# Scaling the first pooled weights by sums of all squares instead of column norms in a hybrid attention and pooling layer

## The chip, the cores and the metric

The kernel runs on one core of one Trainium2 chip. The metric is the device time of one execution in microseconds. Before the change it is 1169.89 us, the median of three runs that lie between 1169.45 and 1170.81.

## The reference

One encoder layer on 4096 tokens of 1024 channels, all in float32:

```
h = rmsnorm(x, pre_norm_g)
[q | k | v | g_a | u_p | g_p] = h @ w_in          # 2304 columns
a = banded_attention(q, k, v, rel_bias, sink) * silu(g_a)   # |i-j| <= 128, 8 heads
p = multiscale_pool(u_p, pool_w, pool_scale) * silu(g_p)    # windows 2, 4, 8, 16
x = x + rmsnorm(concat(a, p) @ w_out, post_norm_g)
```

The change touches how the kernel prepares the weights of `g_p`, the gates of the pooling half (512 columns of `w_in`), and of the normalization of the first tokens.

## The kernel before, in words

**Numbers.** TensorE multiplies float16. Each float32 operand is split into a high and a low float16 half, and a product takes three matmuls (high by high, low by high, high by low). So that the halves keep their accuracy, every group of weight columns is first multiplied by a power of two, `sw`, which is computed on the chip from the weights: `scale_of` (line 192) turns a bound on the squares into that power in four small instructions. The first gain vector has such a power too, `gs`. The inverse powers come back in the factors that evacuations multiply by (`sc`, `isc`, `cg`, `uf`).

**Stages.** The first stage, to about 470 us, projects the tokens in eight blocks of 512 (m = 0 to 7) on the three groups GP (`g_p`), UU (`u_p` with the pooling map folded in) and GA (`g_a`). Block 0 uses plain products: `plain` (line 743) goes over four quarters of operands, A11, A12, A21 and A22, four steps of six matmuls each for each half of the tokens. Later blocks use seven products of sums of those quarters (`quad`, line 777). The later stages (keys, values, queries, attention, output) have a schedule by hand and aren't touched.

**The planner.** In the first stage every operation is a step, `do(engine, cost, due, function, r=..., w=...)`. `Steps.run` (line 86) takes, for the engine that can begin earliest, the step with the smallest due time among those that are ready, adds its cost and a gap of 0.2 us, and so writes one fixed order for every engine. On the chip the engines run in that order, with semaphores between them. Costs and due times are thus only what makes the order. A square of a tile costs `act(D)`, 1.10; a low half `dve(D)`, 1.33.

**The opening.** ScalarE squares the first 256 tokens, transposed, in four chunks (`first_square`, line 416); VectorE adds the chunks in three additions and a fold (`first_add`, `first_fold`, lines 419 to 423); two matmuls with a column of ones sum over the channels (`first_sum`, 425), VectorE adds the epsilon (`first_eps`, 433), GpSimd takes the power -1/2 (`first_root`, 436), TensorE spreads the result over all partitions (`spread`, 442). Then, for each chunk c, VectorE normalizes (`norm_half`, 478: two instructions of 128x256), ScalarE makes the high half (`b_high`, 494) and VectorE the low half (`b_low`, 497).

Ahead of that stands the gain: its largest square is found (`gain_most`, `gain_spread`), and `gain_scale` (394) reduces it, makes `gs`, and scales the gain (`gsc`) and a factor (`gh`).

The weights of GP come in four tiles; tiles 0 and 1 are group "ga" (operands A11 and A12), tiles 2 and 3 group "gb" (A21 and A22). In `norms` (590) ScalarE squares a tile (`w_square`, 567), eight matmuls with ones sum the squares of each of its 128 columns over the 1024 rows (`w_norm`, 573), and `w_scale` (582) takes the largest of the 256 column sums of the group with a reduction of 128x256 (`scale_pow`, 186), makes `sw`, and then `sc` and `isc`. With `sw`, ScalarE writes the high half of each operand (`w_high`, 605) and VectorE the low half (`w_low`, 608). Until weights and tokens are there, TensorE runs idle matmuls (`turn_over`, 402: 52, then 40, then 24 of them).

`gp_flags` (662) later brings both groups of GP to their smaller power, `com`, for the sums of later blocks, and makes the factor `uf` from it. At the end of the first stage `out_scales` (1121) puts `isc` into the rows of the output weights.

The steps of the prediction name these: the "second scale" is that of group "gb"; the "fourth low half of x" is `b_low` of chunk 3.

Of the kernel before, what the change touches and what calls it, by code (L numbers as in the profile page):

```python
# [8 lines left out]
F32 = mybir.dt.float32  # L9
# [8 lines left out]
P = 128  # L18
# [116 lines left out]
def hybrid_layer(ctx: ExitStack, tc, io, out):  # L135
# [75 lines left out]
    with ExitStack() as actx:  # L211
# [55 lines left out]
        def tile_keys(q, si):  # L267
            a = si // 2
            return [f"tile{q}.{si}"] + raw_keys(q, 2 * a) + raw_keys(q, 2 * a + 1)
# [14 lines left out]
        def dve(n):  # L284
            return 0.1 + n * 0.0012
# [11 lines left out]
        def t_scalar(eng, out, in0, s1, op0, s2=None, op1=None):  # L297
            if op1 is None:
                eng.tensor_scalar(out=out, in0=in0, scalar1=s1, scalar2=None, op0=op0)
            else:  # L300
                eng.tensor_scalar(out=out, in0=in0, scalar1=s1, scalar2=s2, op0=op0, op1=op1)
# [89 lines left out]
            bc["g"] = spread_tile(P, 0)  # L391
            nc.tensor.matmul(bc["g"], bc["m"].to_broadcast([P, P]), ident, start=True, stop=True)

        def gain_scale():
            m2 = comm.tile([P, 1], F32, name="m2", tag="m2")
            V.tensor_reduce(out=m2, in_=bc.pop("g"), axis=mybir.AxisListType.X, op=ALU.max)
            scale_of(gs, m2, 1e-30, H_SCALE)
            t_scalar(V, gsc, g_pre, gs, ALU.mult)
            t_scalar(V, gh, gs, 1.0 / H_SCALE, ALU.mult)

# [7 lines left out]
        do("PE", 5.5, -9, turn_over, 52, r=["ones"], w=["bankv", "turned"])  # L408
        do("PE", 0.3, -6, gain_spread, r=["ident", "gmost", "turned"], w=["bc", "spread0"])
        do("PE", 2.3, -6, turn_over, 40, r=["ones", "spread0"], w=["bankv"])  # L410
        do("DVE", 1.4, -6, gain_scale, r=["gpre"], w=["gs", "bc"])


        xsq = NT[:, : 2 * D].rearrange("p (k b t) -> p k b t", k=HK, b=2)
# [107 lines left out]
        for c, d in ((0, 1), (2, 3), (1, 3)):  # L522
            do("DVE", dve(512), -4, first_add, c, d, r=[f"xsq{c}"], w=[f"xsq{d}"])
        do("DVE", dve(256), -4, first_fold, w=["xsq3"])
        do("PE", 0.5, -4, first_sum, r=["onesf", "xsq3"], w=["wup1", "summed"])
        do("DVE", 0.2, -4, first_eps, w=["wup1", "ssq0"])
        do("POOL", 0.8, -3, first_root, slice(0, 2), r=["mhalf", "ssq0"], w=["rs0"])
        for i, t, k in ((2, xn1, "xn"), (3, NT[:, 2 * D : 3 * D], "ts")):
            ld(-2.5 + 0.1 * i, t, x_blk[i], 0.5, w=[k])
# [34 lines left out]

        n2_t = {}

        def w_square(raw, z):
            A.activation(
                sqt[z].rearrange("p (g c) -> p g c", g=2) if len(raw.shape) == 3 else sqt[z], raw,
                AF.Square,  # L570
            )

        def w_norm(z, group, i, n, b):
            if i == 0:
                n2_t[group] = psa.tile([P, n, P], F32, name=f"n2{group}", tag=f"n2{b}")
            for k in range(KT):
                nc.tensor.matmul(
                    n2_t[group][:, i], ones16, sqt[z][:, k * P : (k + 1) * P], start=(k == 0),
                    stop=(k == KT - 1), skip_group_check=True,
                )  # L580
# [9 lines left out]
        def norms(keys, last, views, reads, group, cols):  # L590
            n, b = len(views), turn("n2")
            for i, (key, view, r) in enumerate(zip(keys, views, reads)):
                z = turn("sq")
                do("ACT", act(D), key, w_square, view, z, r=r, w=[f"sqt{z}"])
                do("PE", 0.5, key + 0.5, w_norm, z, group, i, n, b,
                   r=["ones", f"sqt{z}"] + ["summed"] * (group == "ga"), w=[f"n2{b}"])
            do("DVE", 1.5, last, w_scale, group, cols, r=["gs"], w=[f"n2{b}", f"sw{group}"])

        def tile_view(q, i):
            return raws[q][:, 2 * (i // 2) : 2 * (i // 2) + 2, i % 2]  # L600
# [25 lines left out]
        def sum_weights(q, scale, group, key, step, eng, again=False):  # L626
# [8 lines left out]
            if again:  # L635
# [10 lines left out]
            pair(q, S2, 0, scale, key + 2.5 * step, group)  # L646
            pair(q, S4, 1, scale, key + 3.5 * step, group)

        norms([5, 5], 5, [tile_view(GP, i) for i in (0, 1)], [tile_keys(GP, i) for i in (0, 1)],
              "ga", slice(0, 2))  # L650
        do("PE", 1.4, 6, turn_over, 24, r=["ones", "swga"], w=["bankv"])
        do("PE", 0.9, 5.6, row_prod, r=["row", "yt0", "summed"], w=["n20"])
        do("ACT", 0.7, 5.6, row_keep, w=["n20", "yt0"])
        for i, op, key in ((0, A11, 9.5), (1, A12, 12.5)):
            pair(GP, op, i, sw[:, 0:1], key, "ga")
        norms([13, 13], 13, [tile_view(GP, i) for i in (2, 3)], [tile_keys(GP, i) + ["w4h"] * (i == 3) for i in (2, 3)],
              "gb", slice(2, 4))

        def gp_gates():
# [2 lines left out]
        def gp_flags():  # L662
            V.reciprocal(rat, sw[:, 0:4:2])
            tt(V, com, sw[:, 0:1], sw[:, 2:3], ALU.min)
            t_scalar(V, rat, rat, com, ALU.mult)
            t_scalar(V, sc[:, 0:4], com.to_broadcast([P, 4]), gh, ALU.mult)
            V.reciprocal(isc[:, 0:4], sc[:, 0:4])
            w_gates(cg[:, 0:4], slice(0, 4))
            t_scalar(V, uf, sc[:, 0:1], U_EVAC * GP_EVAC * H_SCALE, ALU.mult)

        do("DVE", 0.2, 20, gp_gates, r=["swga", "swgb"] + [f"xb0.{c}.1l" for c in range(HK)], w=["gates"])
        do("DVE", 1.2, 40, gp_flags, r=["swga", "swgb", "gates"], w=["flags", "swgc"])
        for i, op, key in ((2, A21, 16.0), (3, A22, 17.0)):
            pair(GP, op, i, sw[:, 2:3], key, "gb")

# [445 lines left out]
        def out_scales():  # L1121


            tt(V, rowsc[:, 0:4], isc[:, A_GA : A_GA + 4],
               isc[:, SB + B_V : SB + B_V + 1].to_broadcast([P, 4]), ALU.mult)
            tt(V, rowsc[:, 4:8], isc[:, A_GP : A_GP + 4], isc[:, A_U : A_U + 4], ALU.mult)
            t_scalar(V, rowsc[:, 0:4], rowsc[:, 0:4], 2.0**25, ALU.mult)
            stt(rowsc[:, 4:8], rowsc[:, 4:8], 2.0**26, psc, ALU.mult, ALU.mult)

# [1014 lines left out]
```

## Time and profile before

| | |
|---|---|
| median of three runs | 1169.89 us (1169.45 to 1170.81) |
| span of the profiled execution, first to last instruction | 1166.3 us |
| median less that span | 3.6 us |
| TensorE busy | 1150.3 us, 99% of the span |
| VectorE busy | 937.0 us, 80% |
| ScalarE busy | 702.3 us, 60% |
| GpSimd busy | 314.2 us, 27% |
| mean granted clock of TensorE | 0.997 |

The page of the profile gives the span of the profiled execution and no time of its own beside it; what lies around the span is therefore taken as the distance to the median. The lines shown below name, for each group or piece, the engine, the line of the kernel, the operation, what it writes and reads, the shape, and how many there were. In the order of time the first two numbers are the start and the duration of a piece in microseconds; instructions that follow each other without a pause are merged, so a piece of several ends with its last. Square brackets hold the idle time of that engine just before a piece and what ended it. PEld is the loading of weights into TensorE, which overlaps with matmuls. Many lines belong to helpers (299, 307 and 310 are the common VectorE operations), so that an operation is told by its tiles: `xb<-xb,gsc,bc` is a normalization, `xb<-xb,xb` a low half of x, `wq<-wq,sw` on VectorE a low half of weights, on ScalarE a high one.

### The profile page before, as it was taken

The numbers are of one execution on the slowest core, as the hardware profiler recorded it, in microseconds if no ns is written. First come the engines' busy times: TensorE is split into PE (matmuls) and PEld (weight loads), VectorE is DVE, ScalarE is ACT, GpSimd is POOL, SyncE is SP. The second block draws the span as 40 slices with busy tenths as digits, with TensorE's granted clock in tenths as the row PEclk, the third lists the DMA queues.
The fourth block names the chain that finished last, engine by engine and source line by source line (L and its number), as shares of the span: only waits on it lengthen the run. The fifth ranks groups of instructions, "written<-read, shape, count | busy, mean of one in ns | idle before, by whom it ended". The sixth has DMA issues, their size and how long they took to land. (4 is left out here: it accounts for less than half of the span.)

```text
span 1166.3 us, 34144 instructions
## 1 busy us (share of the span) xinstructions
PE 1150.3 (99%) x14380; PEld 885.7 (76%) x14380; DVE 937.0 (80%) x1875; ACT 702.3 (60%) x1460; POOL 314.2 (27%) x310
## 2 busy tenths in 40 slices
PE   7999999999999999999999999999999999999997
PEld 6998888888888888977677676676766767667643
DVE  6889988988799973568877877887887887797786
ACT  6876546546654542267676666666667666666672
POOL 0001121211111010201533433533443443353231
PEclk9999999999999999999999999999999999999999
DMA  9645585867667663399886777787788578677784
GB/s 341 218 127 181 172 271 181 280 217 253 209 193 239 202 173 124 94 277 255 210 201 142 192 194 162 186 187 185 146 191 200 124 204 200 130 196 154 164 234 142
DMA packets 292169, 225.97 MB, mean 194 GB/s; under 512 B 210816, under 2 KB 249984, under 8 KB 287408
## 3 DMA queue, kind: packets, MB, share of 16 engines
q1 hardware_dynamic: 292016, 223.80, 70.1%
q8 instruction: 112, 1.84, 0.7%
q14 instruction: 41, 0.34, 0.1%
HBM read 114.68 MB, written 60.34 MB: 150 GB/s over the span
## 5 line engine op out<-in xcount | busy, mean ns | idle before, releaser
L689 PEld LDWEIGHTS <-wq 128*128 128x128 f16 x4104 | 401.6, 98 | 51.1 <-DVE wq L310 2.9
L689 PE MATMUL y<-xt,wq 128*128 128x256 f16 x1512 | 203.3, 273 | 0.1
L1352 ACT ACTIVATE p<-p,nm 128x385 f32<-128x385 f32 (+1 forms) x256 | 152.9, 599 | 35.2 <-POOL p L1335 20.4
L1273 PE MATMUL aq<-xb,xb 128*128 128x256 f16 x1024 | 173.4, 273 | 0.1
L1634 PE MATMUL ms<-wo,ys 128*128 128x512 f16 x720 | 162.7, 379 | 0.3 <-DVE mo L1673 0.3
L1382 DVE SCALAR_TENSOR_TENSOR pn<-p,rd,pn 128x384 f16<-128x384 f32 (+1 forms) x256 | 157.1, 665 | 5.9 <-ACT pn L1374 5.9
L1341 DVE CUSTOM_DVE_ANT_0 p<-s,nt,nsink 128x384 f32<-128x384 f32 (+1 forms) x256 | 156.0, 667 | 2.1 <-PE s L1318 2.0
L1273 PEld LDWEIGHTS <-xb 128*128 128x128 f16 x1280 | 125.3, 98 | 22.5 <-issue 6.3
L1273 PE MATMUL aq<-xb,xt 128*128 128x256 f16 x512 | 139.5, 273 | 0.0
L1374 ACT ACTIVATE pn<-p,rd 128x384 f16<-128x384 f32 (+1 forms) x256 | 134.5, 596 | 4.2 <-issue 1.1
L307 POOL TENSOR_TENSOR yt<-yt,sg 128x512 f32<-128x512 f32 (+2 forms) x32 | 51.0, 1593 | 301.7 <-DVE yt L310 223.3
L1634 PEld LDWEIGHTS <-ys 128*128 128x128 f16 x720 | 69.2, 98 | 81.6 <-issue 3.1
L1634 PE MATMUL m<-wo,y 128*128 128x512 f16 x540 | 121.8, 379 | 0.0
L1634 PEld LDWEIGHTS <-y 128*128 128x128 f16 x540 | 51.4, 98 | 63.0 <-issue 2.9
L1668 POOL TENSOR_TENSOR mo<-mo,gpost 128x512 f32<-128x512 f32 x39 | 63.8, 1635 | 95.3 <-ACT jkb L1657 94.1
L689 PE MATMUL plain<-xb,wq 128*128 128x256 f16 x576 | 68.0, 276 | 2.8 <-DVE wq L310 2.4
L1273 PEld LDWEIGHTS <-xt 128*128 128x128 f16 x640 | 62.7, 98 | 8.3
L689 PE MATMUL v<-xt,wq 128*128 128x256 f16 x504 | 68.6, 273 | 0.1
L689 PE MATMUL v<-xb,wq 128*128 128x256 f16 x504 | 68.6, 273 | 0.0
L689 PE MATMUL y<-xb,wq 128*128 128x256 f16 x504 | 68.6, 273 | 0.0
L689 PE MATMUL x<-xb,wq 128*128 128x256 f16 x504 | 68.1, 273 | 0.5 <-DVE ubuf L310 0.5
L1484 PEld LDWEIGHTS <-vv 128*64 128x64 f16 (+1 forms) x2256 | 55.1, 109 | 11.4 <-issue 7.1
(218 smaller groups left out, 1928.3 us busy)
## 6 DMA issues: line engine op xcount, KB each, us to landing
nt<-in_xT SPq DMA_DIRECT2D x28, 512.0 KB
x_scr<-xb SPq DMA_DIRECT2D x14, 1024.0 KB
xb<-x_scr SPq DMA_DIRECT2D x14, 1024.0 KB
xr<-in_x SPq DMA_DIRECT2D x28, 512.0 KB
out<-xr SPq DMA_DIRECT2D x28, 512.0 KB
xn<-in_x SPq DMA_DIRECT2D x27, 512.0 KB
ga_scr<-cc SPq DMA_DIRECT2D x64, 128.0 KB
raw<-in_w_out SPq DMA_DIRECT2D x16, 512.0 KB
```

The costliest lines, as they stand in the source:

```text
L307: eng.tensor_tensor(out=out, in0=in0, in1=in1, op=op)
L689: nc.tensor.matmul(b[:, s], wq[:, slot[q, op], wv, s, k, :], x[:, xv, k, :], start=(first and k + s + wv + xv == 0), stop=(last and k == H ...
L1273: nc.tensor.matmul(acc, w[:, j, k, :], x[:, kh, v, kt, :], start=(n == 0), stop=(n == 3 * KT - 1),)
L1341: nc.vector.tensor_tensor_reduce(out=p_t[b, half][:, hh, :nk], in0=s_t[jj][:, gg, :nk], in1=bias[:, h, lo : lo + nk], scale=negc[:, h : h ...
L1352: nc.scalar.activation(p[:, hh, : nk + 1], p[:, hh, : nk + 1], AF.Exp, bias=nm_t[b, half][:, hh : hh + 1], scale=-1.0, accum_out=den_t[b, ...
L1374: nc.scalar.activation(prob_view(b, half)[:, 0, i], p_t[b, half][:, i, :nk], AF.Copy, scale=rd_t[b, half][:, i : i + 1],)
L1382: nc.vector.scalar_tensor_tensor(out=pn4[:, 1, i], in0=p_t[b, half][:, i, :nk], scalar=rd_t[b, half][:, i : i + 1], in1=pn4[:, 0, i], op0= ...
L1484: nc.tensor.matmul(o_t[b][side][a, half], v_t[ku][ks, vi, kt, a], pt[b, half][ks, pi, g, :, kb - kbs[0], (LOW, TOP)[side]], start=start, s ...
L1634: nc.tensor.matmul(z_t[u, tag], y[:, k, yi, :], wo[o][:, wi, k, :], start=(n == 0 and acc is None), stop=(n == 3 * HK - 1), skip_group_che ...
L1668: eng.tensor_tensor(out=mo, in0=mo, in1=gpost[:, cs], op=ALU.mult)
```

## The change

The gain's step is cut in two: `gain_power` (reduction and `gs`) and `gain_scale` (`gsc`, `gh`); the first now waits for the last addition of the tokens' squares, and the second for the epsilon step. Group "ga" and "gb" get `first_norms` in place of `norms`: the square also accumulates each row's sum (`accum_out`), one matmul with ones adds these over the partitions (`w_sum`), and the larger of the two tiles' sums gives the scale (`first_scale`). The column norms are still computed, behind that; their maxima (`w_most`) go into a factor of their own, `scc`, in `gp_flags`, from which `uf` and the output rows are made.

```
-        def gain_scale():
+        def gain_power():
             m2 = comm.tile([P, 1], F32, name="m2", tag="m2")
             V.tensor_reduce(out=m2, in_=bc.pop("g"), axis=mybir.AxisListType.X, op=ALU.max)
             scale_of(gs, m2, 1e-30, H_SCALE)
+
+        def gain_scale():
             t_scalar(V, gsc, g_pre, gs, ALU.mult)
             t_scalar(V, gh, gs, 1.0 / H_SCALE, ALU.mult)
...
-        do("DVE", 1.4, -6, gain_scale, r=["gpre"], w=["gs", "bc"])
...
         do("DVE", dve(256), -4, first_fold, w=["xsq3"])
+        do("DVE", 0.9, -3.9, gain_power, r=["xsq3"], w=["gs0", "bc"])
         do("PE", 0.5, -4, first_sum, r=["onesf", "xsq3"], w=["wup1", "summed"])
-        do("DVE", 0.2, -4, first_eps, w=["wup1", "ssq0"])
+        do("DVE", 0.2, -3.8, first_eps, r=["gs0"], w=["wup1", "ssq0"])
+        do("DVE", 0.4, -3.7, gain_scale, r=["gpre", "gs0", "ssq0"], w=["gs"])
...
+        wsum = pa.tile([P, 4], F32, name="wsum")
+        swc = pa.tile([P, 2], F32, name="swc")
+        scc = pa.tile([P, 1], F32, name="scc")
+
+        def w_square(raw, z, **more):
             A.activation(
                 sqt[z].rearrange("p (g c) -> p g c", g=2) if len(raw.shape) == 3 else sqt[z], raw,
-                AF.Square,
+                AF.Square, **more,
             )
...
+        def w_sum(group, cols, b):
+            n2_t[group] = psa.tile([P, 2, P], F32, name=f"n2{group}", tag=f"n2{b}")
+            bc[group] = psa.tile([P, 2], F32, name=f"ws{group}", tag="wup1")
+            nc.tensor.matmul(bc[group], onesf, wsum[:, cols], start=True, stop=True)
+
+        def w_most(group, j):
+            V.tensor_reduce(
+                out=swc[:, j : j + 1], in_=n2_t.pop(group), axis=mybir.AxisListType.XY, op=ALU.max
+            )
+
+        def first_scale(group, cols):
+            m2 = comm.tile([P, 1], F32, name="m2", tag="m2")
+            V.tensor_reduce(out=m2, in_=bc.pop(group), axis=mybir.AxisListType.X, op=ALU.max)
+            scale_of(sw[:, cols], m2, 1e-20, W_SCALE)
+            t_scalar(V, sc[:, cols], sw[:, cols], gh, ALU.mult)
+            V.reciprocal(isc[:, cols], sc[:, cols])
+
+        def first_norms(keys, last, views, reads, group, cols):
+            b, zs, c = turn("n2"), [], cols.start
+            for i, (key, view, r) in enumerate(zip(keys, views, reads)):
+                zs.append(turn("sq"))
+                do("ACT", act(D) + 0.2, key,
+                   lambda view=view, z=zs[-1], i=i: w_square(
+                       view, z, accum_out=wsum[:, c + i : c + i + 1]),
+                   r=r, w=[f"sqt{zs[-1]}", f"wsum{group}{i}"])
+            do("PE", 0.2, last + 0.5, w_sum, group, cols, b,
+               r=["onesf"] + [f"wsum{group}{i}" for i in range(2)] + ["summed"] * (group == "ga"),
+               w=["wup1", f"n2{b}"])
+            do("DVE", 1.2, last, first_scale, group, cols, r=["gs"], w=["wup1", f"sw{group}"])
+            for i, z in enumerate(zs):
+                do("PE", 0.5, last + 0.6, lambda z=z, i=i: w_norm(z, group, i, 2, None),
+                   r=["ones", f"sqt{z}"], w=[f"n2{b}"])
+            do("DVE", 0.45, 21, w_most, group, c // 2, w=[f"n2{b}", f"swc{group}"])
...
-            t_scalar(V, uf, sc[:, 0:1], U_EVAC * GP_EVAC * H_SCALE, ALU.mult)
+            tt(V, swc[:, 0:1], swc[:, 0:1], swc[:, 1:2], ALU.max)
+            scale_of(scc, swc[:, 0:1], 1e-20, W_SCALE)
+            tt(V, scc, scc, gh, ALU.mult)
+            t_scalar(V, uf, scc, U_EVAC * GP_EVAC * H_SCALE, ALU.mult)
+            V.reciprocal(scc, scc)
...
-        do("DVE", 1.2, 40, gp_flags, r=["swga", "swgb", "gates"], w=["flags", "swgc"])
+        do("DVE", 1.2, 40, gp_flags, r=["swga", "swgb", "swcga", "swcgb", "gates"], w=["flags", "swgc"])
...
-            tt(V, rowsc[:, 4:8], isc[:, A_GP : A_GP + 4], isc[:, A_U : A_U + 4], ALU.mult)
+            tt(V, rowsc[:, 4:8], isc[:, A_U : A_U + 4], scc.to_broadcast([P, 4]), ALU.mult)
```

The two calls of `norms` for groups "ga" and "gb" become calls of `first_norms` with the same arguments.

More of the change, by code (lines that the diff above doesn't have):

```diff
@@ L565, in hybrid_layer @@
         n2_t = {}
-        def w_square(raw, z):
+        wsum = pa.tile([P, 4], F32, name="wsum")
+        swc = pa.tile([P, 2], F32, name="swc")
+        scc = pa.tile([P, 1], F32, name="scc")
+        def w_square(raw, z, **more):
             A.activation(
                 sqt[z].rearrange("p (g c) -> p g c", g=2) if len(raw.shape) == 3 else sqt[z], raw,
-                AF.Square,
+                AF.Square, **more,
             )
         def w_norm(z, group, i, n, b):
-            if i == 0:
+            if i == 0 and group not in n2_t:
                 n2_t[group] = psa.tile([P, n, P], F32, name=f"n2{group}", tag=f"n2{b}")
@@ L647, in sum_weights @@
             pair(q, S4, 1, scale, key + 3.5 * step, group)
-        norms([5, 5], 5, [tile_view(GP, i) for i in (0, 1)], [tile_keys(GP, i) for i in (0, 1)],
+        first_norms([5, 5], 5, [tile_view(GP, i) for i in (0, 1)], [tile_keys(GP, i) for i in (0, 1)],
               "ga", slice(0, 2))
@@ L655, in hybrid_layer @@
             pair(GP, op, i, sw[:, 0:1], key, "ga")
-        norms([13, 13], 13, [tile_view(GP, i) for i in (2, 3)], [tile_keys(GP, i) + ["w4h"] * (i == 3) for i in (2, 3)],
+        first_norms([13, 13], 13, [tile_view(GP, i) for i in (2, 3)], [tile_keys(GP, i) + ["w4h"] * (i == 3) for i in (2, 3)],
               "gb", slice(2, 4))
```

## The prediction

> **What bounds the kernel now.** I read the page first, then the list of what TensorE waited for, then the order of time of each engine from 0 to 40 us, because everything that the change touches lies there.
>
> ```profile
> span 1166.3 us, 34144 instructions
> PE 1150.3 (99%) x14380; PEld 885.7 (76%) x14380; DVE 937.0 (80%) x1875; ACT 702.3 (60%) x1460; POOL 314.2 (27%) x310
> PE plain L689 <- DVE wq L310: 2.4, 1, 2.4
> ```
>
> TensorE is busy for 1150.3 of 1166.3 us. All its idle time is 16 us, and its longest single wait, 2.4 us, is in the opening: the first product waits for the low half of its weights. So the change, which works in the opening, is worth what it shifts the moment from which TensorE never starves again. That moment is in its order of time (start, duration, engine, line, operation):
>
> ```profile
> 7.49 2.40 PE L405 MATMUL idle<-ones 128*128 128x128 bf16 x40
> 14.41 1.50 PE L405 MATMUL idle<-ones 128*128 128x128 bf16 x24
> 16.27 0.28 PE L689 MATMUL plain<-xb,wq 128*128 128x256 f16 x1 [0.36 <-ACT wq L606]
> 18.90 2.42 PE L689 MATMUL plain<-xb,wq 128*128 128x256 f16 x11 [2.35 <-DVE wq L310]
> 21.97 2.37 PE L689 MATMUL plain<-xb,wq 128*128 128x256 f16 x18
> 24.18 0.61 PE L443 MATMUL bc<-ident,rs 128*128 128x128 f32 x4
> 24.63 6.98 PE L689 MATMUL plain<-xb,wq 128*128 128x256 f16 x60
> 26.95 4.37 PEld L689 LDWEIGHTS <-wq 128*128 128x128 f16 x41 [0.37 <-DVE wq L310]
> 56.15 2.78 PE L689 MATMUL plain<-xb,wq 128*128 128x256 f16 x24
> 58.77 0.61 PE L577 MATMUL n2u<-sq,ones 128*128 128x128 bf16 x8
> ```
>
> The dense rate is 24 matmuls from 56.15 to 58.77, 0.109 us each, so one step of six is 0.655 us. The 12 first matmuls (16.27 and 18.90) are steps 0 and 1 of operand A11; the 18 from 21.97 are steps 2 and 3 and step 0 of A12; 18 more of A12 follow the four row spreads, and at 26.95 the first weights of A21 arrive 0.37 us late. 60 matmuls from 24.63 on are 6.5 us at the dense rate, and take that and the 0.37. The stretches of the profile show no idle TensorE after it before 100 us, and then:
>
> ```profile
> 100.00:150.00 50.00, 49.40 (x453) 43.99 (x451) 48.38 (x65) 28.36 (x41) 8.76 (x7) 1.00 0.56 172
> ```
>
> (Columns: stretch and its length, busy time of PE, PEld, DVE, ACT and POOL with the instructions in brackets, clock, DMA share, GB/s.) The mark to move is therefore "A11, A12 and the spreads done, A21 begins": **26.95 us now**. What sets it is VectorE, which hardly pauses from 13.05 on:
>
> ```profile
> 7.21 0.69 DVE L307 TENSOR_TENSOR nt<-nt 128x512 f32<-128x512 f32 x1
> 7.82 0.28 DVE L396 TENSOR_REDUCE m<-sp 128x1 f32<-128x128 f32 x1
> 9.09 1.14 DVE L307 TENSOR_TENSOR nt<-nt 128x512 f32<-128x512 f32 x2
> 10.99 0.16 DVE L299 TENSOR_SCALAR ssq<-sp 128x2 f32<-128x2 f32 x1 [0.76 <-PE sp L428]
> 13.05 0.87 DVE L310 SCALAR_TENSOR_TENSOR xb<-xb,gsc,bc 128x256 f32<-128x256 f32 x2 [1.90 <-PE bc L443]
> 13.85 0.42 DVE L189 TENSOR_REDUCE m<-n2ga 128x1 f32<-128x256 f32 x1
> 14.86 0.17 DVE L209 TENSOR_SCALAR sw<-m 128x2 f32<-128x2 f32 x1
> 15.41 0.67 DVE L307 TENSOR_TENSOR xb<-xb,xb 128x512 f16<-128x512 f32 x1
> 16.00 1.65 DVE L310 SCALAR_TENSOR_TENSOR xb<-xb,gsc,bc 128x256 f32<-128x256 f32 x4
> 17.57 1.28 DVE L310 SCALAR_TENSOR_TENSOR wq<-wq,sw 128x1024 f16<-128x1024 f32 x1
> 18.76 1.29 DVE L307 TENSOR_TENSOR xb<-xb,xb 128x512 f16<-128x512 f32 x2
> 19.96 0.87 DVE L310 SCALAR_TENSOR_TENSOR xb<-xb,gsc,bc 128x256 f32<-128x256 f32 x2
> 20.75 1.28 DVE L310 SCALAR_TENSOR_TENSOR wq<-wq,sw 128x1024 f16<-128x1024 f32 x1
> 21.94 0.69 DVE L307 TENSOR_TENSOR xb<-xb,xb 128x512 f16<-128x512 f32 x1
> 22.55 0.42 DVE L189 TENSOR_REDUCE m<-n2gb 128x1 f32<-128x256 f32 x1
> 25.62 2.48 DVE L310 SCALAR_TENSOR_TENSOR wq<-wq,sw 128x1024 f16<-128x1024 f32 x2
> ```
>
> From start to start: one chunk's normalization (two instructions) 0.79 us, one low half of x 0.61, one low half of weights 1.19, one scale of a group (13.85 to 15.41) 1.56.
>
> **The change part by part.**
>
> *Tokens.* The gain block (7.82 to 9.09) no longer stands ahead of the two additions, so they take 7.82 to 8.97. TensorE still has its 40 idle matmuls (7.49 to 9.89) before the sum of squares, which can begin at 9.9; the epsilon step moves from 10.99 to about 10.5. The reduction and the power of the gain, less than the block's 1.27 us, then lie between 8.97 and 10.25, beside the sum, and cost nothing; if they were longer by a microsecond, the epsilon behind them would only lose what it won. The gain's two scalings follow it and end near 11. The root on POOL comes 0.5 us earlier. No DMA is issued by any moved step, and SP's queue keeps its order.
>
> *The first scale.*
>
> ```profile
> 10.75 1.06 ACT L568 ACTIVATE sq<-wq 128x1024 bf16<-128x1024 f32 x1 [1.06 <-DMA wq<-in_w_a]
> 15.07 2.19 ACT L606 ACTIVATE wq<-wq,sw 128x1024 f16<-128x1024 f32 x2 [0.48 <-DVE sw L209]
> 19.17 1.04 ACT L319 ACTIVATE xn<-xn 128x1024 f32<-128x1024 f32 x1
> 20.12 0.18 ACT L319 ACTIVATION_READ_ACCUMULATOR xn<-xn 128x1 f32 x1
> 261.51 0.28 PE L1034 MATMUL tn<-total,onesf 128*128 128x1 f32 x2
> 6.95 0.16 DVE L387 TENSOR_REDUCE m<-g 128x1 f32<-128x8 f32 x1
> ```
>
> The second tile's square still begins when its DMA lands, 10.75. A square with an accumulator takes 19.17 to 20.30, 1.13 us, so its sum is there at 11.9 (not 11.8). The matmul over two columns has its like in the 0.28 us one of the projections: 12.2. The reduction of 128x2 in PSUM isn't in the trace; its bounds are 0.16 (128x8) and 0.28 (128x128, above), and I take 0.16, the nearer size. With it the scale block takes 1.30 instead of 1.56 us: 12.2 to 13.5, its `sw` at about 13.2 instead of 15.03. That is 1.8 us won, but not all of it passes on:
>
> - The block now stands ahead of the first normalization on VectorE, which begins at 13.5 instead of 13.05. Its spread of the root would be there at 13.25, behind the sum, and one column norm, on TensorE. Half a microsecond is lost there.
> - On ScalarE the due times put the third tile's square between `sw` and the first high half: it starts when the first column norm has released its buffer (12.7) and ends at 13.85. The high half begins there, 1.2 us before 15.07.
>
> VectorE then goes on in the order that the planner's costs give: three normalizations (13.54 to 15.91), the low half of A11 to 17.10, three low halves of x to 18.95, the fourth normalization to 19.75, the low half of A12 to **20.95**, where it now is at 21.94. One microsecond won: 0.26 from the shorter block, and some 0.8 because VectorE opens this chain with the scale block at 12.2 and not with the normalization at 13.05.
>
> *The second scale.* It also is shorter by 0.26 us, but its place decides. By hand through the planner (its costs and gaps, which set the order and no time): VectorE is free after the low half of A12 at 20.8 of planned time, the second group's scale is open at 20.2, the fourth low half of x only at 21.1, because its high half waits on ScalarE behind the square of token block 2. So the planner writes the scale first, 1.30 us, and the engine runs in that order: 20.95, scale to 22.25, fourth low half of x to **22.85**. Now that is done at 22.55, when the next instruction begins. So step 3 of A11 comes 0.3 us later than now, although everything else is earlier. From there TensorE has step 3 (0.655), the spreads (0.45 to the next start), and all four steps of A12 (2.62): 22.9 + 3.7 = **26.6**. A21's scale is known at 22.0, its low half ends near 24.95 even behind the two column-norm maxima; it doesn't wait. Against 26.95 the gain is **0.35 us**.
>
> *Added work.* The two sums on TensorE (0.28 each) and the column norms fall into its pauses. The two maxima (0.42 each by the 13.85 row) and eight small instructions with the flags (about 1.3 us at the 0.17 of the 14.86 row) come to VectorE, less the 0.5 us saved in the blocks. They are covered by its pauses behind 45 us:
>
> ```profile
> 47.66 0.75 DVE L299 TENSOR_SCALAR wq<-wq,rat 128x2048 f16<-128x2048 f16 x1 [2.20 <-PE plain L689]
> 60.56 1.28 DVE L310 SCALAR_TENSOR_TENSOR wq<-wq,com 128x1024 f16<-128x1024 f32 x1 [3.47 <-ACT wq L606]
> ```
>
> 5.7 us of cover for 1.7 us. Without it TensorE could wait up to 1.7 us between 100 and 150, where VectorE is busy for 48.38 of 50 us.
>
> **Sum.** Span 1166.3 - 0.35 = 1165.95. The median of the runs, 1169.89, lies 3.6 us above the profiled span; I keep that distance: 1169.5. Between the bounds of the reduction, and with half a microsecond for the order, the gain is -0.3 to 0.9.
>
> **The rivals.**
>
> 1. *The clock takes it back (slower).* In the present run the clock fell after the long wait:
>
> ```profile
> 19.00:19.25 0.25, 0.25 (x3) 0.60 1.05 420
> 22.25:22.50 0.25, 0.25 (x3) 0.57 1.04 426
> ```
>
> These are the first and the last of 14 quarter microseconds (busy PE, then the clock), all between them at 0.50: half a clock from 19.05 to 22.46, 3.4 us, behind a wait of 2.35 us. Now that costs nothing, since VectorE is the limit until 26.9. In the changed kernel the waits are spread: some 1.4 us before 17.1 and 2 us before 22.9, after the column norms. If the second one lowers the clock, the 3.4 us fall on dense work and 1.7 us are lost: 1169.5 + 1.7 = 1171.2. Past 1172.2 it goes only where the wait is also longer than worked out. For it: 2.35 us were enough once. Against it: a good third of any 3.4 us around the new wait is matmuls, while of the 3.4 us before 19.05 only about 0.7 us was (the end of the 24 idle ones, the one at 16.27, the first behind 18.90). The Trainium skill (TensorE: Matmul & The Clock Gate, Part 1: The HAM clock gate) says the clock halves after a whole idle window of about 3.4 us, free-running; by that rule no wait here would do it, and the time would stay at 1169.5. The trace agrees on the 3.4 us and not on the whole window: a matmul of 0.28 us stood in it. Chance 0.17.
>
> 2. *The fourth low half of x goes ahead of the second scale (faster).* The order hangs on 0.3 us of planned time. Then it ends at 21.55, step 3 and A12 run 21.6 to 25.3, and A21's low half is ready by 25: a gain of 1.65 us, 1168.2. Chance 0.16. To pass 0.2% the opening would have to win 2.3 us, and A21's own low half, not before 24.95, caps it at 2.0.
>
> 3. *The rest of the plan is reshuffled.* Earlier steps change what is open when, up to 470 us. TensorE has only 0.6 us of waits in 100 to 150 to win, and VectorE, 48.38 of 50 us busy there, to lose: -0.6 to +2 us, 1169 to 1171.5. Chance 0.10.
>
> 4. *The change doesn't bring the scale forward,* because the DMA of the second tile at 10.75 and the buffer of the squares hold it: 1169.9. It shares its side with the forecast. Chance 0.05.
>
> **How the numbers follow.** The forecast has 0.52. About 0.2%, 2.3 us, is what a measurement of this kernel can tell from no change. The forecast, rivals 2 and 4, most of 1 and of 3 stay within: 0.83. Slower by more: a third of rival 1 and a little of 3, 0.09. Faster by more: an order that I worked out wrongly in more than one place, which lifts that cap as well, 0.08. The range reaches from below rival 2 (1168.2, less the 0.7 us that the runs scatter) to above rival 1 (1171.2, with the same): 1167.4 to 1171.9.
>
> **What would show it.** Right: first `sw` near 13.2, first high half near 13.9, low half of A12 ending near 21, then the second scale, then the last low half of x ending near 22.9; A21's first matmul behind A12 without a wait near 26.6; the same operations from 60 us on about 0.3 us earlier. Wrong: the last low half of x before the second scale (rival 2), a clock of 0.5 on the steps of A12 (rival 1), a new wait of TensorE behind 60 us (rival 3).

## The result and the profile after

The changed kernel takes **1172.63 us** (median of six, 1171.63 to 1173.91), the kernel before in the same comparison 1169.37 (six, 1168.24 to 1170.81): ratio **1.0033, interval 1.0022 to 1.0045**. It is slower by 3.3 us, more than the 0.2% that the prediction took as the least that can be told from no change, and the time lies outside the range (1167.4 to 1171.9).

Span and waits of TensorE after (engine, line, what it waited for, us in total, times, longest):

```profile
span 1172.1 us, 34144 instructions
```
```profile
PE o L1529 <- DMA pt<-pn: 2.9, 2, 1.6
PE v L734 <- DVE cc L307: 2.6, 3, 1.9
PE plain L734 <- DVE xb L307: 2.2, 2, 1.9
PE fp L353 <- DMA yt<-in_onehot: 2.2, 1, 2.2
PE x L734 <- DVE ubuf L310: 1.2, 1, 1.2
```

The spans differ by 5.8 us, the medians by 3.3: in every run here the time is 1.8 us over the span, so the profile after (1173.91) is the slowest of its six, and the one before (1166.3 + 1.8 = 1168.1) lies 1.3 us under its median.

What is new in the waits stands in two places. The `fp` and `plain` rows lie in the opening. The `v` and `x` rows lie at 126.8, 229, 289.6 and 334 us, where nothing of the change is. Busy TensorE between 30 and 480 us, before and after:

```profile
sum 450.00, PE 449.28; mean PE 89.86
```
```profile
sum 450.00, PE 446.19; mean PE 89.24
```

It is idle for 0.72 us before and 3.81 after, at the full clock. The first `aq` product, the mark at which the next stage begins, moves from 490.09 to 494.74: 4.65 us, of which 3.1 are these waits and the other 1.5 the opening of this profile. The remaining 1.2 us of the spans lie behind that mark; the wait `pt<-pn` alone grew by 1.1 (1.8 before, 2.9 now).

The opening, TensorE:

```profile
12.37 1.01 PE L353 MATMUL fp<-yt,rbias 32*8 32x512 f32 x2 [2.22 <-DMA yt<-in_onehot]
13.31 0.38 PE L609 MATMUL wsga<-wsum,onesf 128*128 128x2 f32 x2
14.20 1.17 PE L444 MATMUL bc<-ident,rs 128*128 128x128 f32 x4
24.79 0.60 PE L734 MATMUL plain<-xb,wq 128*128 128x256 f16 x4 [1.93 <-DVE xb L307]
25.67 4.53 PE L734 MATMUL plain<-xb,wq 128*128 128x256 f16 x40
```

the second tile's square on ScalarE:

```profile
11.86 1.06 ACT L575 ACTIVATE sq<-wq 128x1024 bf16<-128x1024 f32 x1 [0.23 <-DMA wq<-in_w_a]
```

and VectorE:

```profile
10.18 0.16 DVE L299 TENSOR_SCALAR ssq<-sp 128x2 f32<-128x2 f32 x1 [0.26 <-PE sp L429]
13.73 0.16 DVE L618 TENSOR_REDUCE m<-wsga 128x1 f32<-128x2 f32 x1 [3.20 <-PE wsga L609]
14.49 0.17 DVE L209 TENSOR_SCALAR sw<-m 128x2 f32<-128x2 f32 x1
22.74 0.15 DVE L618 TENSOR_REDUCE m<-wsgb 128x1 f32<-128x2 f32 x1
24.06 0.67 DVE L307 TENSOR_TENSOR xb<-xb,xb 128x512 f16<-128x512 f32 x1
24.65 0.42 DVE L612 TENSOR_REDUCE swc<-n2ga 128x1 f32<-128x256 f32 x1
25.31 2.47 DVE L310 SCALAR_TENSOR_TENSOR wq<-wq,sw 128x1024 f16<-128x1024 f32 x2
```

`fp` (`row_prod`) is the product of the relative bias with a one-hot table. In the new order it stands ahead of `wsga`, the sum that the first scale needs (`w_sum`), and TensorE waits 2.22 us for the table's DMA. Little of that wait reaches `wsga`: the second square began only at 11.86, when its own DMA landed, 1.1 us later than in before's profile (10.75), so its sum is there at 13.0, and `wsga` begins 0.3 us behind that. The first `sw` begins at 14.49 instead of 14.86, 0.4 us earlier and not 1.8. A12 then begins at 25.67; its 24 products at 0.109 us put the start of A21 at 28.3, 1.3 us later than before's 26.95. This pair of profiles can't say how much of the 1.3 us the order makes: in late_four (below), whose opening is before's, the second square began at 11.83 and A12 at 26.04.

Near 125 us, TensorE and VectorE of the changed kernel:

```profile
123.46 0.82 PE L734 MATMUL v<-xb,wq 128*128 128x256 f16 x6
124.12 0.82 PE L734 MATMUL y<-xt,wq 128*128 128x256 f16 x6
126.81 0.81 PE L734 MATMUL v<-xt,wq 128*128 128x256 f16 x6 [1.87 <-DVE cc L307]
```
```profile
123.12 1.22 DVE L307 TENSOR_TENSOR xt<-nt,xt 128x1024 f16<-128x1024 f32 x1
124.26 1.24 DVE L953 COPY ubuf<-ubuf 128x64 f32<-128x64 f32 x1
125.42 0.73 DVE L310 SCALAR_TENSOR_TENSOR nt<-nt,gsc,bc 128x512 f32<-128x512 f32 x1
126.08 0.68 DVE L307 TENSOR_TENSOR cc<-v,cc 128x512 f32<-128x512 f32 x1
```

(`v`, `x` and `y` are banks in which TensorE sums its products.) The bank `v` is finished at 124.3 and wanted again one product group later, at 124.94; VectorE, which has no pause here, adds it into `cc` behind a halo copy and a normalization. In the kernel before, two groups lay between, `y` at 123.55 and `x`:

```profile
122.60 0.82 PE L689 MATMUL v<-xb,wq 128*128 128x256 f16 x6
124.84 0.81 PE L689 MATMUL x<-xb,wq 128*128 128x256 f16 x6 [0.48 <-DVE ubuf L310]
125.49 0.82 PE L689 MATMUL v<-xt,wq 128*128 128x256 f16 x6
```
```profile
124.71 0.68 DVE L307 TENSOR_TENSOR cc<-v,cc 128x512 f32<-128x512 f32 x1
```

There the addition begins 1.3 us behind the end of `v` (1.8 in the changed kernel), and `v` is asked for only once it is free.

### The profile page after: what moved, and what is told of

Same layout as the page of the kernel before. It is cut to its first block, busy times and chain, and to the rows that moved or that the text cites. A ratio compares the mean times of both kernels' runs of the same rounds, so it can differ in the third digit from the quotient of the medians.

```text
span 1172.1 us, 34144 instructions
## 1 busy us (share of the span) xinstructions
PE 1151.3 (98%) x14384; PEld 886.6 (76%) x14384; DVE 937.7 (80%) x1884; ACT 704.3 (60%) x1464; POOL 317.7 (27%) x310
## 5 line engine op out<-in xcount | busy, mean ns | idle before, releaser
L307 POOL TENSOR_TENSOR yt<-yt,sg 128x512 f32<-128x512 f32 (+2 forms) x32 | 53.6, 1674 | 290.7 <-DVE yt L310 228.5
L842 ACT COPY cc<-y 128x512 f32<-128x512 f32 x42 | 24.6, 585 | 78.9 <-PE y L734 77.8
```

The costliest lines, as they stand in the source:

```text
L307: eng.tensor_tensor(out=out, in0=in0, in1=in1, op=op)
L842: A.copy(dst, bank_t[bk])
```

## The experiments

All but gap_19 use one handle. The order in which the planner's steps are written out is given as a list; each engine's queue is its own part of that list. The steps themselves stay as they are, but for gain_only, which has a part of the change:

```
-        for n in sorted(range(n_steps), key=lambda n: (begun[n], n)):
+        for n in ORDER:
```

Theory A: the loss is made by the order that the planner wrote anew, above all far behind the change. Theory B: the change's instructions or its shorter scale cost the time themselves. "Behind 30 us" is meant in planned time. Times are medians beside the kernel before of the same comparison (1168.4 to 1168.8).

**Which stretch of the order.** *h1_opening*: the changed kernel, its own order up to 30 us, before's order behind.

```
 # after.py
+ORDER = steps planned before 30 us as after has them, the rest as before has them
```

> The changed kernel's opening alone: its steps in the order that its planner wrote up to 30 us of planned time, and behind that every step in the order of the kernel before. Theory A (the rewritten order of the rest costs the time, in waits of TensorE near 125, 220, 290 and 330 us): within 1.3 us of the kernel before, and no wait of TensorE over 1 us between 60 and 400 us. Theory B (the opening itself costs it: the wait for the one-hot table, the second scale ahead of the fourth low half of x): 2.5 to 4 us slower than the kernel before. Theory C (the arrival of the first loads scatters from run to run, and the profiles of before and after were a fast and a slow one): as A in the median, but with A21's first matmul anywhere between 26.5 and 28.5 us.

1170.72, ratio 1.0015 (1.0005 to 1.0024), 2.0 us over: between the 1.3 us that Theory A allowed and the 2.5 that B asked for. Of the waits between 60 and 480 us only before's 0.5 us is left.

*h2_rest*: the kernel before, not one instruction changed, its own opening and the changed kernel's order behind 30 us.

```
 # before.py
+ORDER = steps planned before 30 us as before has them, the rest as after has them
```

> The kernel before, with its own opening (all steps up to 30 us of planned time), and behind that the order that the changed kernel's planner wrote; not one instruction is another than before. Theory A: 2.5 to 3.5 us slower than the kernel before, with the waits of TensorE for VectorE near 125, 220, 290 and 330 us. Theory B: within 0.7 us of the kernel before. Theory C: within 1 us.

1171.78, 1.0026 (1.0017 to 1.0035), with the waits of the changed kernel (`v<-cc` 2.6 us, `x<-ubuf` 1.2). So a loss of nearly that size needs none of the change's instructions. *h2_mid* and *h2_late* cut this once more, at 70 us:

```
 # h2_mid
+ORDER = after's order for the steps planned from 30 to 70 us, else before's
 # h2_late
+ORDER = before's order up to 70 us, after's behind
```

> The kernel before, with the changed planner's order only for the steps that were planned between 30 and 70 us; ahead of it and behind it the order of the kernel before. If the wait of 1.9 us near 125 us comes from what this stretch puts later (the second square of token block 1, its root and its spread), that wait stays, and those at 220, 290 and 330 us go: 1 to 2 us slower than the kernel before. If it comes from the order behind 70 us: within 0.7 us of the kernel before.

> The other part: the kernel before, with the changed planner's order only for the steps planned behind 70 us. By the first account the wait near 125 us goes and those at 220, 290 and 330 us stay, some 1.5 us of them: 1 to 2 us slower. By the second all 3.8 us of waits stay: 2.5 to 3.5 us slower.

h2_mid 1169.17, 1.0002 (0.9992 to 1.0013); h2_late 1172.3, **1.0029** (1.0017 to 1.0041), TensorE idle 3.81 us between 30 and 480 as in the changed kernel. *gain_only* and *h2_square_back* look at single edits:

```
 # gain_only: before.py with the cut gain step, the additions ahead of it; before's order behind 30 us
 # h2_square_back: h2_rest, one step of ScalarE (a square of block 1) back ahead of a high half
-    w_high[2,0], square[1,1]
+    square[1,1], w_high[2,0]
```

> The kernel before with the change's first part alone (the additions of the tokens' squares ahead of the scale of the gain, which is cut in two), the old column norms, and the order of the kernel before behind 30 us. The epsilon near 10.5 instead of 11.0 us and the first normalization 0 to 0.4 us earlier, later only where the product with the one-hot table, now right behind the tokens' sum, waits for its load. 0 to 0.5 us faster, within what can be measured the same; if the table lands late here too, 0 to 0.7 us slower.

> The kernel before with the changed planner's order behind 30 us, as measured, but for one step: the square of token block 1's second part stands again ahead of the high half of a weight on ScalarE, where the kernel before has it, and not behind that and a gate. If this one step's place makes the wait near 125 us: the square at 40 instead of 42.7 us, the spread of block 1 near 62.7 instead of 64.4, the wait near 125 at most 0.6 instead of 1.9, and 1 to 1.5 us less than that kernel's 3.0 us over the kernel before. If the wait has another cause, it stays at 1.9.

gain_only 1168.62, 1.0000 (0.9991 to 1.0009). h2_square_back 1172.46, 1.0030 (1.0020 to 1.0040): the square came 3.6 us sooner and the 1.87 us wait stayed, so that account falls.

**The opening.** Two steps stand in other places than before: the one-hot product ahead of the sum, and the second scale ahead of the fourth low half of x. *h1_low_first* puts the second back, *h1_row_late* the first (with the copy and store that it feeds), *h1_both* both; *h1_again* is h1_opening once more.

```
 # h1_low_first
-    VectorE: second scale, fourth low half of x
+    VectorE: fourth low half of x, second scale
 # h1_row_late
-    TensorE: one-hot product, w_sum, column norms
+    TensorE: w_sum, column norms, one-hot product
```

> As the first of these runs, with the fourth low half of x ahead of the second group's scale on VectorE. By rival 2 of the prediction step 3 of A11 comes about 1.3 us earlier, and the whole 0.9 to 1.3 us under the first run of this call. If the opening doesn't pass its start on to the end, no difference to the first run.

> As the third of these runs, and the product with the one-hot table behind the two column norms of the first group instead of ahead of the sum. Where that table lands late, TensorE's sum no longer waits for it: first scale up to 0.5 us earlier than in the third run, 0 to 0.5 us off the time, about 1 us below the kernel before if the order of the rest is what cost the time.

> The kernel of h1_opening once more. Its ratio was 1.0015, but in its profile the first aq product begins at 490.38, only 0.29 us later than before's, while the stretch behind it is 3.0 us longer: a wait of 1.94 us (before 1.01) for a DMA near 537, and half the clock for 3.3 us after it. If that is how this order usually runs, the profile again shows a wait of 1.6 us or more near 537 with the clock at 0.5 behind it, and the time is 1170.5 or over. If it was chance, the profile shows a wait near 1.0 to 1.3 without the fall and a time of 1168 to 1169.5; if the opening's own lateness differs from run to run, the first aq product begins at 491 or later.

> h1_opening with the one-hot product (and what it feeds) behind both column norms, the second scale still ahead of the fourth low half of x. If the one-hot wait is what the opening's order costs, the ratio falls to 0.9995 to 1.0006 and the first aq product begins at 490.1 or earlier. If the place of the second scale is, the ratio stays at 1.001 or over. With h1_low_first (1.0012, the other half of h1_both) this is the fourth corner of the square.

| ratio to before | second scale ahead | fourth low half ahead |
|---|---|---|
| one-hot product ahead | 1.0015 (1.0005-1.0024), 1.0014 (1.0005-1.0023) | 1.0012 (1.0003-1.0021) |
| one-hot product behind | 1.0000 (0.9992-1.0008) | 0.9999 (0.9990-1.0008) |

The place of the one-hot product, moved together with its copy on ScalarE and its store on SP's queue, carries it; which of the three was not separated, and the product's own delay of `w_sum` is only the 0.3 us above. The place of the second scale cannot be told from nothing. In h1_both TensorE waits for the square's sum and then goes on at once:

```profile
11.50 0.38 PE L685 MATMUL wsga<-wsum,onesf 128*128 128x2 f32 x2 [1.37 <-ACT sq L651]
23.91 6.28 PE L810 MATMUL plain<-xb,wq 128*128 128x256 f16 x56
```

Its first `sw` begins at 12.68 and A12 at 23.91, 0.7 us before the old kernel's 24.63 (its second square began 0.45 us sooner as well, at 10.30). All the change's instructions are in this run, and it takes 1168.65: Theory B falls, and so does any gain. The first `aq` product is at 489.92, 0.17 us earlier.

Where the 1.7 us of the table's upper row pass to the end is less plain. The first `aq` product begins only 0.3 us later than before in h1_opening and 1.0 in h1_again. Part of h1_again's 1.0 us goes with half a clock on products of A11, from 18.6 to 22.1 us:

```profile
18.75 3.51 PE L810 MATMUL plain<-xb,wq 128*128 128x256 f16 x16 [0.31 <-DVE xb L383]
```

The same 16 take 1.91 us in h1_opening. In after_four (below), which has the changed kernel's opening, half a clock lies on step 3 of A11 and on A12, from 23.9 to 27.3:

```profile
24.00:24.25 0.25, 0.25 (x3) 0.50 1.04 393
```

That is the fall of rival 1. The three profiles with the one-hot product behind (h1_both, h1_row_late, after_six) have none on A11 or A12, but how often it comes cannot be told from single profiles. In both runs of h1_opening's kernel the rest arises behind the first `aq` product, at a wait for a DMA; h1_again, and the clock in 1 us stretches:

```profile
540.64 0.25 PE L1605 MATMUL o<-pt,vv 128*64 128x128 f16 x2 [2.89 <-DMA pt<-pn]
542.67 3.55 PE L1755 MATMUL m<-wo,y 128*128 128x512 f16 x12
```
```profile
541.00:542.00 1.00, 1.00 (x25) 0.50 0.90 324
543.00:544.00 1.00, 1.00 (x4) 0.50 1.28 291
```

The kernel before:

```profile
536.77 0.25 PE L1484 MATMUL o<-pt,vv 128*64 128x128 f16 x2 [1.01 <-DMA pt<-pn]
538.02 2.76 PE L1634 MATMUL m<-wo,y 128*128 128x512 f16 x12
```

The wait is 2.89 us instead of 1.01, and half a clock from about 540.9 to 544.3 follows. In h1_opening it is 1.94 with the same fall; in h1_both 1.05 and in h1_row_late 0.85 without. h1_low_first had 1.21 and no fall in a profiled run of 1168.56, one of the fastest of its eleven. So the fall near 540 us is seen twice, but why this DMA comes later when the one-hot product stands earlier was not settled.

**The wait near 125 us.** Is TensorE's order asking too early, or VectorE's order too late? *late_vector* and *late_tensor* put one engine's steps between 66 and 140 us back into before's order, *late_cc* moves one step, *late_band* takes the new order for 70 to 140 us alone. A rank is a step's place in its engine's queue.

```
 # late_vector: h2_late, VectorE's queue from 66 to 140 us as before has it (24 ranks)
 # late_tensor: h2_late, TensorE's queue from 66 to 140 us as before has it (91 ranks)
 # late_cc: h2_late, one step of VectorE
-    t_low, halo copy, norm, add v into cc, add x into u
+    t_low, add v into cc, halo copy, norm, add x into u
 # late_band: before.py, after's order from 70 to 140 us only
```

> Before's instructions, the changed kernel's order of all engines behind 70 us, but VectorE's steps planned at 66 to 140 us stand in before's order (24 positions of VectorE's queue; no other queue is touched). At 122.63 TensorE of h2_late asks for the bank v one product group (0.65 us) after the last product in it, and VectorE adds that bank into cc only at 123.92. Account T (TensorE's order asks too early): in before's order VectorE adds the bank at 124.71, later still, so the wait near 125 stays at 1.9 us or grows to 2.7, and the time stays at 1172 to 1173. Account V (VectorE lost 1.4 us waiting for the evacuation of UU at 92 and 1.8 us beside GpSimd because the gates' window sums were placed earlier): the wait near 125 falls under 0.7 us and the time by 1.2 us, to about 1171.

> As h2_late, but TensorE's steps planned at 66 to 140 us stand in before's order (91 positions of TensorE's queue, no other queue). Account T: three more groups (2 us) lie between the last product in the bank v and the next use of it, so the 1.87 us wait near 125 is gone or under 0.6 us; the other waits (0.3 us near 225, 1.2 near 290, 0.5 near 330) stay, and the time falls by 1.3 us, to about 1171. Account V: the wait stays over 1.3 us, since VectorE is as late as it was.

> As h2_late with one step moved: VectorE's addition of the bank v into cc (at 123.92) stands three places earlier, behind the xt step that ends at 122.1 and ahead of the halo copy (1.25 us) and a normalizing product (0.74 us). Account T: the addition runs at 122.2 to 122.9 and the wait near 125 shrinks from 1.87 to 0.3 to 0.5 us; the copy and the product behind it run 0.7 us later, which can give up to 0.7 us back a few us on. Time 0.8 to 1.5 us below h2_late. Account V: the same by this step, since it takes the lateness away however it came; so this run prices one step's place and does not separate the two.

> Before's instructions; the changed kernel's order for the steps planned at 70 to 140 us alone, before's in front and behind. If each wait is made by the order in its own place: the 1.9 us wait near 125 is there, those near 225, 290 and 330 are not, and the time is 1.4 us over before (1170.1, ratio 1.0012). If the lateness made near 125 brings on the later ones, they are there too and the time is that of h2_late (1172.3).

*late_vector* is the slowest kernel of the study, 1175.53, 1.0056 (1.0042 to 1.0070): with before's VectorE order under the new TensorE order the wait grows.

```profile
118.91 0.81 PE L765 MATMUL v<-xb,wq 128*128 128x256 f16 x6 [0.76 <-DVE cc L383]
127.60 1.22 PE L765 MATMUL v<-xt,wq 128*128 128x256 f16 x6 [3.29 <-DVE cc L383]
```

*late_tensor*, 1172.94, 1.0036 (1.0023 to 1.0049): the wait for `v` is gone, and three others stand in its place, 1.96 us together.

```profile
115.34 0.81 PE L765 MATMUL y<-xt,wq 128*128 128x256 f16 x6 [0.41 <-ACT cc L871]
116.76 0.81 PE L765 MATMUL y<-xt,wq 128*128 128x256 f16 x6 [0.60 <-ACT cc L873]
126.66 0.83 PE L765 MATMUL x<-xb,wq 128*128 128x256 f16 x6 [0.95 <-DVE ubuf L386]
```

So TensorE's and VectorE's orders belong together: before's VectorE order under the new TensorE order is worse than h2_late (1.0029), and the new VectorE order under before's TensorE order is no better. *late_cc*, 1170.03, **1.0013** (1.0004 to 1.0022), one step moved ahead of two others:

```profile
122.65 0.69 DVE L383 TENSOR_TENSOR cc<-v,cc 128x512 f32<-128x512 f32 x1
```
```profile
122.45 0.82 PE L765 MATMUL y<-xt,wq 128*128 128x256 f16 x6
123.39 0.81 PE L765 MATMUL v<-xt,wq 128*128 128x256 f16 x6
```

The next `v` product follows 0.94 us behind the start of the group before it, the dense rate being 0.655. Against h2_late that is 0.16% for a wait of 1.9 us; the two intervals overlap (h2_late 1.0017 to 1.0041). *late_band*, 1169.5, 1.0004 (0.9995 to 1.0013), has the wait (1.88 us at 125.21) and none of the later ones, and starts `aq` 1.0 us late: the later waits are made in their own places, not handed on from the first. But 1.0012 was expected of it. The same wait alone in before's order costs 0.13% at most by its interval, and may cost nothing; so the 0.16% of late_cc is not a fixed price of such a wait.

**Does a handful of steps account for it?** *late_four* moves three more steps of VectorE, those behind which TensorE waits near 226, 287 and 332 us; *after_four* does the same in the changed kernel, *after_six* adds h1_both's two moves. *gap_19* changes a number of the planner that no instruction carries.

```
 # late_four, after_four: late_cc's move and
-    fourth window sums (block 2), add v into cc
+    add v into cc, fourth window sums (block 2)
-    t_sums, b_low, halo copy, add x into u
+    t_sums, halo copy, add x into u, b_low
-    fourth window sums (block 4), add v into cc
+    add v into cc, fourth window sums (block 4)
 # gap_19: before.py
-    GAP = 0.2
+    GAP = 0.19
```

> h2_late (before's instructions, the changed kernel's order behind 70 us) with four steps of VectorE moved: the addition of the bank v ahead of the halo copy near 125 us (as in late_cc), the one near 225 us and the one near 330 us ahead of the window sums of the fourth gate tile, and the UU step near 287 us ahead of one xb step. If the loss sits in the place of these steps alone, all waits of TensorE between 60 and 480 us are under 0.3 us each and the time is 1168.5 to 1169.2 (ratio 0.9998 to 1.0006). If something else in the new order costs time, the ratio stays at 1.001 or over, as late_cc's was 1.0013.

> The changed kernel itself, its whole order kept, with the same four steps moved. Its opening is as it was, so what is left is what h1_opening showed: ratio 1.0010 to 1.0018 (1169.8 to 1170.6) against 1.0033 for the changed kernel. If the opening and the late part feed each other, it stays over 1.002.

> after_four with the opening's two moves of h1_both as well: the one-hot product behind both column norms, the fourth low half of x ahead of the second scale. All of the changed kernel's instructions in all but its own order, a handful of steps moved. Expected 1168.3 to 1169.0, ratio 0.9996 to 1.0004: no slower than before, and not faster either, since what the first scale's earlier start is worth was 0.14 to 0.18 us of lead at block 1's first spread. If the added instructions cost something of their own, the ratio is 1.001 or over.

> Before, with one constant of the planner changed: the gap that it puts behind each step, 0.20 to 0.19 us. No instruction changes; the order does, but not in the opening. If each rewriting of the late order is a draw of its own, the time can land anywhere from 1168 to 1172, with new waits of TensorE where it is over 1169.5. If before's order is not special and only the changed kernel's was unlucky, it is 1168.2 to 1169.2, without new waits.

late_four misses: 1170.99, 1.0018 (1.0009 to 1.0027), no better than late_cc. The waits aimed at are gone, and two new ones have come:

```profile
236.50 0.82 PE L765 MATMUL v<-xt,wq 128*128 128x256 f16 x6 [1.09 <-DVE cc L383]
289.73 1.47 PE L765 MATMUL y<-xt,wq 128*128 128x256 f16 x12 [0.66 <-ACT cc L871]
```

1.75 us in place of 1.94. after_four 1170.81, 1.0017 (1.0007 to 1.0028), against 1.0033 without the moves; after_six 1170.23, 1.0014 (1.0005 to 1.0022), with the same two waits, not the 1.0004 at most that was expected. So here moving three more steps only traded three waits for two. gap_19 gives 1169.25, 0.9999 (0.9991 to 1.0008), without a new wait between 60 and 480 us: not every rewriting of the order costs (this one changes the rank of 251 of TensorE's 723 steps, h2_late's of 520); the changed kernel's did.

No kernel here beats the one before. The change's instructions in before's order behind 30 us, with the two moves in the opening (h1_both), equal it within 0.1%.

## Why the prediction was wrong

1. *Tokens.* Right for the times: epsilon at 10.18 (10.5 forecast), the gain's steps hidden. Wrong in "SP's queue keeps its order": the store of the bias row, fed by the one-hot product, stands ahead of four loads that it followed before, at 21.84 instead of 26.43.
2. *First scale.* The sizes were right (reduction of two columns 0.16, sum 0.28 to 0.38), its start was not. The prediction took `w_sum` at 11.9, behind the square's sum. It began at 13.31: 1.1 us later because the second tile's DMA landed later in this profile, and 0.3 us because of the one-hot product, which the text never named among what is queued ahead on TensorE. In h1_both, where that product stands elsewhere and the tile landed sooner, `w_sum` starts at 11.50 and `sw` is done at 12.85, better than the 13.2 forecast.
3. *Second scale ahead of the fourth low half.* The order was as worked out (22.74, then 24.06 against 22.25 forecast for the end of the scale), later by that start and by spreads at half the clock; its cost to the end is within the uncertainty of the square above.
4. *A21 at 26.6.* It is 28.3: in this profile a loss of 1.3 us where 0.35 of gain stood, with 1.1 us of later loads in it.
5. *Added work.* Its two maxima don't lie in the pauses behind 45 us but at 24.65, ahead of A21's low halves; these end at 27.8, still 0.5 us before A21 begins. The whole cost is within h1_both's interval.
6. *Rival 1.* In the changed kernel's profile the clock did fall (below), but onto column norms and spreads, not onto A12. In after_four's, with the same opening, it fell onto A12, where the rival put it. Its part in the median was not measured.
7. *The step that failed:* "the same operations from 60 us on about 0.3 us earlier", and with it rival 3, at a chance of 0.10 and a price of -0.6 to +2 us. A gain in the opening was carried to the end by shifting the old order as a whole. But the planner writes the order from the ready times; h2_late changes the rank of 520 of TensorE's 723 steps and 221 of VectorE's 385. The new order alone costs 1.0029, some 3.4 us, over the upper price. The prediction had the number that should have raised it, VectorE 48.38 of 50 us busy from 100 to 150: VectorE then has little slack to free a bank for which TensorE asks one group sooner.
8. *The distance of 3.6 us from span to median.* It is 1.8 in every run; the profiled execution was a low one.

That the order, and not an instruction, makes the loss is shown (h2_late, h1_both). In the new order, moving one step took 1.0029 to 1.0013 (late_cc), but that this one wait makes half the loss by itself is not shown: late_band has it at 1.0004. The two parts don't add either, 1.0029 late and 1.0015 in the opening against 1.0033 together. How the opening's 1.0015 reaches the end is seen in part in three profiles and not explained.

## What to carry to other kernels

Where an order is written by a planner from costs and due times, an edit at the start is two edits: what it does, and a new order for everything behind. Before its instructions are blamed or praised, run the old instructions in the new order and the new ones in the old; here that took two kernels and turned the question round. And look for what is queued ahead of a step on its in-order engine, above all one that waits for a DMA; a step that is ready sooner gains nothing behind it.

## What the runs showed of the hardware

*Half the clock after waits of 2 us.* In the changed kernel the wait of 2.22 us for the one-hot table is followed by

```profile
14.00:14.25 0.25, 0.25 (x5) 0.50 1.05 393
17.00:17.25 0.25, 0.25 (x5) 0.63 1.08 442
```

and the four spreads behind it take 1.17 us, against 0.71 for before's at 12.31. In h1_both a wait of 1.37 us (the `wsga` row above) was enough:

```profile
12.00:12.50 0.50, 0.50 (x8) 0.50 1.07 406
```

while gap_19 kept the full clock behind a longer one:

```profile
PE plain L689 <- DVE wq L310: 2.3, 1, 2.3
```

The wait of 1.93 us ahead of step 3 shows both: the full clock behind it in the changed kernel (24.79), half a clock in after_four (23.68, the row further up), with the same order of the opening. So the length of a wait does not decide alone; each fall that was seen lasted some 3.4 us. The Trainium skill (TensorE: Matmul & The Clock Gate, Part 1: The HAM clock gate) has the clock drop after at least one idle window of about 3.4 us, and the windows run free of the program. The length and the chance in it agree, the whole idle window does not: the longest wait in front of a fall was 3.29 us (late_vector), and in late_tensor a fall began at 11.8 us behind single waits of 0.51 and 0.27.

*VectorE stands beside GpSimd.* In h2_late, VectorE, then GpSimd (the gate's product):

```profile
94.70 2.53 DVE L383 TENSOR_TENSOR nt<-nt 128x512 f32<-128x512 f32 x3
113.97 1.60 DVE L383 TENSOR_TENSOR nt<-nt 128x512 f32<-128x512 f32 x3
```
```profile
94.87 1.63 POOL L383 TENSOR_TENSOR yt<-yt,sg 128x504 f32<-128x504 f32 x1 [2.54 <-DVE yt L386]
```

Three additions of the same shape take 0.9 us longer when the gate runs beside them, a cost of the order that the planner's costs don't hold. The Trainium skill (SBUF — State Buffer, SBUF: two separate sides) says why that can be: a VectorE operation with two SBUF inputs and one of GpSimd take turns at a shared port pair. The rows agree.

*First loads scatter.* The second tile's square began between 9.48 (h2_square_back) and 11.86 us (the changed kernel) in the profiles of these kernels, and up to 11.83 (late_four) in those with before's opening. A forecast of a tenth of a microsecond in the opening is finer than that.
